# A second way to project sixteen meta tokens on TensorE, and one matmul for the router's sums

## The chip, the cores and the metric

The kernel runs on one core of one Trainium2 chip. The metric is the device time of one launch in microseconds. The kernel before takes 712.66 us (median of 3 runs, 712.54 to 715.22). The core has TensorE (PE, with its weight loads shown apart as PEld), VectorE (DVE), ScalarE (ACT), GpSimd (POOL) and SyncE (SP, which here only issues DMAs).

## The reference, cut to what matters

The model is one layer: 16 meta tokens are put in front of 512 tokens, all are projected by `w_in` (1024 x 3584) to seven groups of 512 columns, two mixers (a gated recurrence and a stick-breaking attention) work on these, an output projection and a layer norm follow, and a routed mixture of 16 experts with a second layer norm ends it.

```
h = concatenate([meta, x])                      # 16 + 512 rows of 1024, float32
proj = h @ w_in                                 # hq, hf, hi, hg, sq, sk, sv: 512 columns each
...
logits_g = xf @ w_rg + b_rg ;  logits_e = xf @ w_re + b_re     # xf: layer norm of the mixers' output
```

Of the meta tokens only four groups are used: hf (forget gates), hi (called hv in the kernel, the recurrence's values), sk and sv (attention keys and values). Outputs for the meta rows are dropped.

For the router, the kernel multiplies rows that are not yet normalised: with g and b the norm's gain and offset, it needs for each of the 20 logits the sum over the 1024 rows of b times the weight (added to the bias, tile `lgb`) and the sum over the rows of g times the weight (tile `nws`, to take off the mean). These two sums of 20 numbers, spread to all 128 partitions, are the "router's sums".

## The kernel before, in words

**Projections.** `projections` (L333 to L369) goes through the seven groups in the order hf, hq, hg, hv, sk, sv, sq. A group's weights come as two loads of 1 MB (`load_w`, the first group's in halves; raw tiles `raws`), each 1024 rows of contraction being 8 blocks (k = 0 to 7) of 128. Since one float32r pass rounds its operands, ACT makes a rounded copy of the weights (L329) and DVE or POOL the rest that is left (L124, L122 in `lo_sub`); x is split likewise (L200, L201). A product is then three float32r matmuls of 128 x 128 by 128 x 512: L128, L129 and L130 in `mm3`. For each k, four accumulators (pool `pj`, 4 banks of PSUM) get their three matmuls each.

**Meta tokens.** Their transposed values `xm` are the weights (stationary operand) of a matmul of their own, in 128 columns: columns 0 to 15 hold the rounded values, 32 to 47 the rest, the other columns zero. For each k of a group that needs them, L359 multiplies by the rounded weights and L360 by the rest of the weights, 512 moving columns each, into one bank of the pool `z`. At the group's end ACT copies partitions 32 to 47 (L366), DVE adds partitions 0 to 15 (L367), and a small routine stores the 16 rows: hf (L429) and sk (L382) by four transposes, hv by a copy on DVE, sv by one float32 matmul with `rep` (L413).

**Weaving.** After 27 steps (three groups) the remaining steps of the projections are woven with the recurrence's heads (`hg_head`), which use the pools `z`, `tr` and `oT`. The order on each engine is made by a scheduler from the order of the code and from what each instruction waits for; on the chip each engine goes through its list in order. Then follow the attention, woven with the output projection, the router, and 16 experts whose 96 MB of weights are streamed by SP.

**Router's sums.** `router_constants` (L303 to L321) runs among the projections. For the offset's sum, eight float32 matmuls (L315) have a column of b spread over 128 columns as weights and 20 moving columns; for the gain's sum, eight (L320) have a matrix of ones as weights and the scaled router weights as moving columns.

A float32 matmul that is not float32r shows as two records in the trace, each with a weight load of its own; a float32r matmul shows as one.

Of the kernel before, what the change touches and what calls it, by code (L numbers as in the profile page):

```python
# [9 lines left out]
F32 = mybir.dt.float32  # L10
F32R = mybir.dt.float32r
BF = mybir.dt.bfloat16
I32 = mybir.dt.int32
AF = mybir.ActivationFunctionType
OP = mybir.AluOpType
AX = mybir.AxisListType
PSUM = bass.MemoryType.PSUM

P = 128
D = 1024  # L20
T = 512
NM = 16
NT = T // P
KC = D // P
# [57 lines left out]
def hymba_kernel(ctx: ExitStack, tc: tile.TileContext, x, meta, w_in, lbnd, hgg, sbg, w_out, ln1g, ln1b,  # L82
                 wrg, brg, wre, bre, wg, wu, wd, ln2g, ln2b, out):
    nc = tc.nc
    V = nc.vector
# [4 lines left out]
    def f32(ap):  # L90
        return ap.bitcast(F32)
# [4 lines left out]
    const = ctx.enter_context(tc.tile_pool(name="const", bufs=1))  # L96
# [4 lines left out]
    def bank(tag, bufs, shape):  # L101
        return ps.tile(shape or [P, 512], F32, tag=tag, bufs=bufs, name=tag)
# [3 lines left out]
    trb = lambda shape=None: bank("tr", 1, shape)  # L106
# [7 lines left out]
    def big_tile(k, dt=F32, pool=None):  # L114
        return (pool or big).tile([P, 2048], dt, tag="b", name="b").rearrange("p (k n) -> p k n", k=k)
# [26 lines left out]
    att = ax_.enter_context(tc.tile_pool(name="att", bufs=1, side="right"))  # L142


    ident = const.tile([P, P], F32, name="ident")
# [10 lines left out]
    ones = upool.tile([P, P], F32, tag="ones", bufs=1, name="ones")  # L156
# [5 lines left out]
    def tt(tag="t", bufs=T_BUFS, n=528, parts=P):  # L162
        return att.tile([P, 528], F32, tag=tag, bufs=bufs, name=tag)[0:parts, 0:n]
# [8 lines left out]
    raws = {}  # L172
# [6 lines left out]
            nc.sync.dma_start(t[:, j * w:j * w + w], rap(w_in, (4 * half + j * w) * P * 3584 + GROUPS[n] * 512,  # L179
                                                         [[3584, P], [P * 3584, w], [1, 512]]))  # L180

    xm = big_tile(2, F32R)[:, 0].rearrange("p (k n) -> p k n", k=KC)
    nc.gpsimd.memset(f32(xm[:]), 0.0)
    mt = big_tile(2)[0:NM, 0, :]
    nc.scalar.dma_start(mt, meta)
    xr = [big_tile(2) for _ in range(2)]
# [4 lines left out]
    for i2 in range(2):  # L191
        xr_ = xr[i2]
        for i1 in range(2):
            i = 2 * i2 + i1
            for hf in range(2):
                p_ = pj([P, 4, P])
                for k in range(4):
                    nc.tensor.transpose(p_[:, k, :], xr_[:, i1, (4 * hf + k) * P:(4 * hf + k + 1) * P], ident)
                d_ = slice(i * P, (i + 1) * P)
                nc.scalar.activation(xhi_[hf][:, :, d_], p_, AF.Copy)  # L200
                x_last = V.tensor_sub(xlo_[hf][:, :, d_], p_, f32(xhi_[hf][:, :, d_])).ins  # L201
    p_ = trb([P, KC, NM])
    for k in range(KC):
        nc.tensor.transpose(p_[:, k, :], mt[:, k * P:(k + 1) * P], ident[:NM, :NM])
    nc.scalar.activation(xm[:, :, 0:NM], p_, AF.Copy)
    V.tensor_sub(xm[:, :, 32:32 + NM], p_, f32(xm[:, :, 0:NM]))

    prm = upool.tile([32, P], F32, tag="prm", bufs=1, name="prm")
    cp = const.tile([P, 32], F32, name="cp")
# [10 lines left out]
    for m in (16, 8, 4, 2, 1):  # L220
        t = upool.tile([P, P], I32, tag=f"lm{m}", bufs=1, name=f"lm{m}")
# [8 lines left out]
        lmask[m] = t  # L230
    identb = att.tile([P, P], BF, name="identb")
    maskb = att.tile([P, P], BF, name="maskb")
    rep = att.tile([NM, 8, NM], F32, name="rep")

    def bcast_row(t, src, eng):
        eng.dma_start(t, rap(src, 0, [[0, P], [1, D]]))
# [23 lines left out]
    wr, lgb, nws = small("wr", [KC, 20]), small("lgb", [20]), small("nws", [20])  # L260
# [22 lines left out]
    def feature_constants():  # L283
        V.tensor_copy(identb, ident)
        nc.gpsimd.memset(maskb, 0.0)
        nc.gpsimd.affine_select(out=maskb, in_=maskb, pattern=[[-1, P]], compare_op=OP.is_ge, fill=MASKED, base=-1,
                                channel_multiplier=1)
        V.tensor_copy(rep, ident[:NM, None, :NM].to_broadcast([NM, 8, NM]))
        for o, src, n in ((0, lbnd, 8), (8, hgg, 4), (12, sbg, 4), (16, ln1g, 8), (24, ln1b, 8)):
            nc.scalar.dma_start(prm[o:o + n], rap(src, 0, [[P, n], [1, P]]))  # L290
        p_ = trb([P, 32])
        nc.tensor.transpose(p_, prm, ident[:32, :32])
        V.tensor_copy(cp, p_)
        V.tensor_max(lbw[:, 0], cp[:, 0:4], cp[:, 4:8])
        V.tensor_sub(lbw[:, 1], cp[:, 0:4], lbw[:, 0])
        V.tensor_sub(lbw[:, 2], cp[:, 4:8], lbw[:, 0])
        nc.scalar.activation(lbw[:, 1:3], lbw[:, 1:3], AF.Exp)
        V.tensor_add(lbw[:, 2], lbw[:, 1], lbw[:, 2])
        V.reciprocal(lbw[:, 2], lbw[:, 2])
        V.tensor_mul(lbw[:, 3], lbw[:, 1], lbw[:, 2])  # L300
        V.tensor_scalar(lbw[:, 4], lbw[:, 3], -1.0, 1.0, op0=OP.mult, op1=OP.add)

    def router_constants():  # L303
        nc.gpsimd.iota(vt[:, :, 0], pattern=[[0, NT]], base=1, channel_multiplier=1, allow_small_or_imprecise_dtypes=True)
        nc.gpsimd.iota(vt[:, :, 1], pattern=[[P, NT]], base=0, channel_multiplier=0, allow_small_or_imprecise_dtypes=True)
        for j in range(2):
            V.tensor_copy(vals[:, :, :, j], vt[:, :, j:j + 1].to_broadcast([P, NT, NE]))
        nc.scalar.dma_start(wr[:, :, 0:4], rap(wrg, 0, [[4, P], [P * 4, KC], [1, 4]]))
        nc.scalar.dma_start(wr[:, :, 4:20], rap(wre, 0, [[16, P], [P * 16, KC], [1, 16]]))

        nc.scalar.dma_start(lgb[:, 0:4], rap(brg, 0, [[0, P], [1, 4]]))
        nc.scalar.dma_start(lgb[:, 4:20], rap(bre, 0, [[0, P], [1, 16]]))
        p_ = trb([P, 20])
        for k in range(KC):
            nc.tensor.matmul(p_, cp[:, 24 + k:25 + k].to_broadcast([P, P]), wr[:, k, :], start=(k == 0), stop=(k == KC - 1))  # L315
        V.tensor_add(lgb, p_, lgb)
        V.tensor_mul(wr, wr, cp[:, 16:24][:, :, None].to_broadcast([P, KC, 20]))
        p_ = trb([P, 20])
        for k in range(KC):
            nc.tensor.matmul(p_, ones, wr[:, k, :], start=(k == 0), stop=(k == KC - 1))  # L320
        V.tensor_scalar(nws, p_, -1.0, None, op0=OP.mult)  # L321


    latest = [None]
# [8 lines left out]
    def projections(uses):  # L333

        wt = {(0, 0): split_w(0, 0)}
        for n, (dmajor, evac, meta_evac) in enumerate(uses):
            acc = [pj() for _ in range(4)]
            pm = zb() if meta_evac else None
            for kk in range(4):
                if kk % 2 == 0 and n + 1 < len(uses):  # L340
                    load_w(n + 1, kk // 2)
                for k2 in range(2):
                    if k2 == 0:
                        whi, wlo = wt.pop((n, kk))
                        nxt = (n, kk + 1) if kk < 3 else (n + 1, 0)
                        if nxt[0] < len(uses):
                            wt[nxt] = split_w(*nxt)
                    k = 2 * kk + k2
                    wfl = slice(k2 * 512, (k2 + 1) * 512)
                    for c in range(4):  # L350
                        wsl = slice(k2 * 512 + c * P, k2 * 512 + (c + 1) * P)
                        xsl = slice(c * P, (c + 1) * P)
                        if dmajor:
                            mm3(acc[c], (whi[:, wsl], wlo[:, wsl]), (xhi[k], xlo[k]), k == 0, k == KC - 1)
                        else:
                            mm3(acc[c], (xhi[k][:, xsl], xlo[k][:, xsl]), (whi[:, wfl], wlo[:, wfl]),
                                k == 0, k == KC - 1)
                    if pm is not None:
                        nc.tensor.matmul(pm, xm[:, k, :], whi[:, wfl], start=(k == 0), stop=False)  # L359
                        nc.tensor.matmul(pm, xm[:, k, :], wlo[:, wfl], start=False, stop=(k == KC - 1))  # L360
                    yield 1
            for c in range(4):
                evac(c, acc[c])
            if pm is not None:
                t = tt(n=512, parts=NM)
                nc.scalar.activation(t, pm[32:32 + NM, :], AF.Copy)  # L366
                V.tensor_add(t, pm[0:NM, :], t)  # L367
                meta_evac(t)
            yield 1  # L369

# [8 lines left out]
    def mev_sk(t):  # L379
        p_ = trb([P, 4, NM])  # L380
        for c in range(4):
            nc.tensor.transpose(p_[:, c, :], t[:, c * P:(c + 1) * P], ident[:NM, :NM])  # L382
        for c in range(4):
            V.tensor_copy(skT[c][:, 0:NM], p_[:, c, :])

# [32 lines left out]
    hvm = ut(n=T)[0:NM]  # L418
# [7 lines left out]
    def mev_hf(t):  # L426
        p_ = trb([P, 4, NM])
        for h in range(4):
            nc.tensor.transpose(p_[:, h, :], t[:, h * P:(h + 1) * P], ident[:NM, :NM])  # L429
        for h in range(4):  # L430
            nc.scalar.activation(bt[h][:, 0:NM], p_[:, h, :], AF.Sigmoid)
            nc.scalar.activation(kt[h][:, 0:NM], p_[:, h, :], AF.Sigmoid, scale=-1.0)
# [10 lines left out]
        nc.scalar.activation(hvt[i], acc, AF.Copy)  # L443

    def mev_hv(t):
        V.tensor_copy(hvm, t)

    def ev_hg(h, acc):
        gt.append(ut(n=T))
# [406 lines left out]
    parts = []  # L856
    for e in range(NE):
        n = 4 if e == NE - 1 else 2 if e >= E_EARLY else 8
# [357 lines left out]
    for hf in range(2):  # L1216
        first_rows(hf, 0)
        p_ = p1_[hf]
# [67 lines left out]
    for e in range(NE):  # L1286
# [15 lines left out]
        if e == last - 1:  # L1302
            rr = []
            for i in range(0, NT, 2):
                t = big_tile(2)
# [170 lines left out]
```

## Time and profile before

| | before |
|---|---|
| median of 3 runs | 712.66 us |
| the profiled execution's own time | 715.65 us |
| its span, first to last instruction | 713.9 us |
| busy: PE / DVE / ACT / POOL | 661.7 / 525.2 / 412.3 / 155.0 us |
| mean granted clock of TensorE, share of full | 0.976 |

The profile is of one execution, which is 3.0 us above the median of the runs; 1.75 us of it lie around the span. A matmul's record is longer than the distance to the next one, because matmuls are pipelined: a record of 0.39 us is followed by the next after 0.23 us. What a matmul costs in a dense stretch is therefore the distance between starts, not the duration.

### The profile page before, as it was taken

The numbers are of one execution on the slowest core, as the hardware profiler recorded it, in microseconds if no ns is written. First come the engines' busy times: TensorE is split into PE (matmuls) and PEld (weight loads), VectorE is DVE, ScalarE is ACT, GpSimd is POOL, SyncE is SP. The second block draws the span as 40 slices with busy tenths as digits, with TensorE's granted clock in tenths as the row PEclk, the third lists the DMA queues.
The fourth block names the chain that finished last, engine by engine and source line by source line (L and its number), as shares of the span: only waits on it lengthen the run. The fifth ranks groups of instructions, "written<-read, shape, count | busy, mean of one in ns | idle before, by whom it ended". The sixth has DMA issues, their size and how long they took to land. (4 is left out here: it accounts for less than half of the span.)

```text
span 713.9 us, 9327 instructions
## 1 busy us (share of the span) xinstructions
PE 661.7 (93%) x3350; PEld 528.6 (74%) x3350; DVE 525.2 (74%) x833; ACT 412.3 (58%) x624; POOL 155.0 (22%) x177
## 2 busy tenths in 40 slices
PE   6999999999999999989977699999999999999963
PEld 5878878777877777778766588888778788787632
DVE  5433064666465696989877899999999999899384
ACT  5353253525262683856433587768688687697570
POOL 5201143343334100100011021413211141112201
PEclk9999999999999999999998799999999999999987
DMA  9431111030003790213576589999999999999631
GB/s 349 129 121 59 60 60 39 22 118 1 1 1 110 275 381 1 67 52 118 156 316 241 188 295 351 350 327 358 339 337 352 320 361 328 346 367 354 212 131 58
DMA packets 62307, 143.67 MB, mean 201 GB/s; under 512 B 7370, under 2 KB 7402, under 8 KB 62256
## 3 DMA queue, kind: packets, MB, share of 16 engines
q1 hardware_dynamic: 53312, 127.93, 49.6%
q0 software_dynamic: 5904, 12.82, 6.2%
q10 hardware_dynamic: 3040, 2.27, 1.0%
q8 instruction: 28, 0.46, 0.3%
q14 instruction: 23, 0.19, 0.1%
HBM read 137.01 MB, written 14.68 MB: 212 GB/s over the span
## 5 line engine op out<-in xcount | busy, mean ns | idle before, releaser
L908 DVE TENSOR_TENSOR b<-b 128x1024 fp32r<-128x1024 f32 x180 | 211.2, 1217 | 8.6 <-ACT b L907 8.1
L907 ACT ACTIVATE b<-b 128x1024 fp32r<-128x1024 f32 x180 | 177.3, 1054 | 13.2 <-SPq L1121 7.7
L128 PE MATMUL pj<-b 128*128 128x512 f32 x256 | 104.4, 411 | 0.3
L129 PE MATMUL pj<-b 128*128 128x512 f32 x256 | 101.9, 398 | 0.6 <-DVE b L124 0.6
L130 PE MATMUL pj<-b 128*128 128x512 f32 x256 | 102.5, 400 | 0.0
L128 PE MATMUL pj<-b,xh 128*128 128x512 f32 x224 | 89.9, 403 | 0.2 <-ACT b L907 0.2
L129 PE MATMUL pj<-b,xl 128*128 128x512 f32 x224 | 88.0, 394 | 0.0
L130 PE MATMUL pj<-b,xh 128*128 128x512 f32 x224 | 86.8, 403 | 0.5 <-DVE b L908 0.5
L974 POOL DMA_INDIRECT xg<-h1d,idx x15 | 20.3, 1354 | 184.3 <-DVE gate L971 82.7
L124 DVE TENSOR_TENSOR b<-b 128x1024 fp32r<-128x1024 f32 x24 | 33.1, 1392 | 33.8 <-ACT b L329 30.2
L128 PEld LDWEIGHTS pj<-b 128*128 128x128 f32 x256 | 48.9, 192 | 10.8 <-DVE b L201 0.7
L130 PEld LDWEIGHTS pj<-b 128*128 128x128 f32 x256 | 48.7, 190 | 10.8 <-issue 0.7
L129 PEld LDWEIGHTS pj<-b 128*128 128x128 f32 x256 | 48.9, 191 | 10.4 <-DVE b L124 0.9
L130 PEld LDWEIGHTS pj<-b,xh 128*128 128x128 f32 x224 | 42.3, 189 | 11.3 <-DVE b L908 2.6
L128 PEld LDWEIGHTS pj<-b,xh 128*128 128x128 f32 x224 | 42.5, 190 | 8.9 <-ACT b L907 1.5
L129 PEld LDWEIGHTS pj<-b,xl 128*128 128x128 f32 x224 | 42.6, 190 | 8.7
L329 ACT ACTIVATE b<-b 128x1024 fp32r<-128x1024 f32 x28 | 29.1, 1051 | 33.8 <-PE pj L130 15.2
L1021 POOL DMA_INDIRECT ad<-y,idx x14 | 39.2, 2802 | 42.7 <-ACT b L907 29.4
L626 ACT ACTIVATE zs<-zs 128x512 f32<-128x512 f32 x28 | 17.7, 631 | 49.1 <-POOL zs L625 49.0
L122 POOL TENSOR_TENSOR b<-b 128x1024 fp32r<-128x1024 f32 x8 | 19.4, 2430 | 91.9 <-ACT b L329 72.3
L624 POOL TENSOR_TENSOR zs<-u 128x256 f32<-128x256 f32 x28 | 22.2, 791 | 63.3 <-issue 25.8
L627 DVE TENSOR_TENSOR zs<-zs,u 128x256 f32<-128x256 f32 x28 | 13.3, 474 | 24.6 <-ACT zs L626 24.6
(357 smaller groups left out, 1310.9 us busy)
## 6 DMA issues: line engine op xcount, KB each, us to landing
b<-in_w_exp_gate_dram SPq DMA_DIRECT2D x32, 1024.0 KB, 8.7
b<-in_w_exp_up_dram SPq DMA_DIRECT2D x32, 1024.0 KB, 9.5
b<-in_w_exp_down_dram SPq DMA_DIRECT2D x32, 1024.0 KB, 8.3
b<-in_w_in_dram SPq DMA_DIRECT2D x12, 1024.0 KB, 5.2
b<-in_x_dram SPq DMA_DIRECT2D x8, 512.0 KB, 7.5
b<-in_w_out_dram SPq DMA_DIRECT2D x4, 1024.0 KB, 4.7
b<-in_w_in_dram SPq DMA_DIRECT2D x4, 512.0 KB
h1d<-b POOLq DMA_DIRECT2D x4, 512.0 KB, 3.0
```

Source lines behind the costliest of these rows:

```text
L122: nc.gpsimd.tensor_sub(dst, src, hi)
L124: V.tensor_sub(dst, src, hi)
L128: nc.tensor.matmul(acc, ah, bh, start=first, stop=False)
L129: nc.tensor.matmul(acc, al, bh, start=False, stop=False)
L130: nc.tensor.matmul(acc, ah, bl, start=False, stop=last)
L329: latest[0] = nc.scalar.activation(wt[:, 0], src, AF.Copy).ins
L624: nc.gpsimd.tensor_sub(xv[:, :, 0, :], ref, bv[:, :, 0, :])
L626: nc.scalar.activation(X, X, AF.Exp)
L907: latest[:] = (nc.scalar.activation(t[:, 0], raw, AF.Copy).ins, V.tensor_sub(t[:, 1], raw, f32(t[:, 0])).ins)
L908: V.tensor_sub(t[:, 1], raw, f32(t[:, 0])).ins)
L974: nc.gpsimd.indirect_dma_start(out=dst, out_offset=None, in_=h1d, in_offset=bass.IndirectOffsetOnAxis(ap=idx, axis=0), bounds_check=T - 1, ...
L1021: nc.gpsimd.indirect_dma_start(out=ad, out_offset=bass.IndirectOffsetOnAxis(ap=idx, axis=0), in_=y, in_offset=None, bounds_check=T - 1, oo ...
```

## The change

The meta tokens' weights `xm` become a float32 tile of 128 x 8 x 32 in the constants' pool (columns 16 to 31 of each block are zero), and no longer take one of the 14 buffers of the pool `big`. L359 and L360 go. Instead, after k = 3 and after k = 7, four float32 matmuls are issued, one for each of the last four k: 32 columns of weights, the raw float32 weights of the group as 512 moving columns, and each of the four writes its own 32 partitions of the bank (0, 32, 64, 96). So the four blocks' sums stand below each other, and are added only when the 16 rows are stored: ACT copies the whole 128 partitions, and the routine of each group multiplies by `fold`, a 128 x 16 matrix with ones where the row is i, 16 + i, 32 + i and so on. hf and sk then have four float32 matmuls in place of four transposes, hv has a matmul of 512 columns and a copy, sv keeps its one matmul with a `rep` of 128 rows in place of 16.

The router's sums over the eight row blocks are made on DVE (two products of 160 columns, two reductions), and one float32 matmul with the matrix of ones and 40 moving columns sums over the partitions.

```diff
-    xm = big_tile(2, F32R)[:, 0].rearrange("p (k n) -> p k n", k=KC)
+    xm = const.tile([P, KC, 32], F32, name="xm")
...
+    rep = att.tile([P, 8, NM], F32, name="rep")
+    fold = rep[:, 0, :]
+    V.tensor_reduce(fold, ident.rearrange("p (j i) -> p i j", i=NM), axis=AX.X, op=OP.add)
+    V.tensor_copy(rep[:, 1:8], rep[:, 0:1].to_broadcast([P, 7, NM]))
...
     nc.scalar.activation(xm[:, :, 0:NM], p_, AF.Copy)
-    V.tensor_sub(xm[:, :, 32:32 + NM], p_, f32(xm[:, :, 0:NM]))
...
-        for k in range(KC):
-            nc.tensor.matmul(p_, cp[:, 24 + k:25 + k].to_broadcast([P, P]), wr[:, k, :], start=(k == 0), stop=(k == KC - 1))
-        V.tensor_add(lgb, p_, lgb)
+        wb = tt(n=40 + KC * 20)
+        w_ = wb[:, 40:].rearrange("p (k n) -> p k n", k=KC)
+        V.tensor_mul(w_, wr, cp[:, 24:32][:, :, None].to_broadcast([P, KC, 20]))
+        V.tensor_reduce(wb[:, 0:20], w_.rearrange("p k n -> p n k"), axis=AX.X, op=OP.add)
         V.tensor_mul(wr, wr, cp[:, 16:24][:, :, None].to_broadcast([P, KC, 20]))
-        p_ = trb([P, 20])
-        for k in range(KC):
-            nc.tensor.matmul(p_, ones, wr[:, k, :], start=(k == 0), stop=(k == KC - 1))
-        V.tensor_scalar(nws, p_, -1.0, None, op0=OP.mult)
+        V.tensor_reduce(wb[:, 20:40], wr.rearrange("p k n -> p n k"), axis=AX.X, op=OP.add)
+        p_ = trb([P, 40])
+        nc.tensor.matmul(p_, ones, wb[:, 0:40], start=True, stop=True)
...
-                    if pm is not None:
-                        nc.tensor.matmul(pm, xm[:, k, :], whi[:, wfl], start=(k == 0), stop=False)
-                        nc.tensor.matmul(pm, xm[:, k, :], wlo[:, wfl], start=False, stop=(k == KC - 1))
+                    if pm is not None and k % 4 == 3:
+                        for j in range(4):
+                            nc.tensor.matmul(pm[32 * j:32 * j + 32], xm[:, k - 3 + j, :], raws[n, k // 4][:, j],
+                                             start=(k == 3), stop=(k == 7), skip_group_check=True)
...
-                t = tt(n=512, parts=NM)
-                nc.scalar.activation(t, pm[32:32 + NM, :], AF.Copy)
-                V.tensor_add(t, pm[0:NM, :], t)
+                t = tt(n=512)
+                nc.scalar.activation(t, pm, AF.Copy)
...
-            nc.tensor.transpose(p_[:, c, :], t[:, c * P:(c + 1) * P], ident[:NM, :NM])
+            nc.tensor.matmul(p_[:, c, :], t[:, c * P:(c + 1) * P], fold, start=True, stop=True)
...
     def mev_hv(t):
-        V.tensor_copy(hvm, t)
+        p_ = trb([P, 512])
+        nc.tensor.matmul(p_[0:NM], fold, t, start=True, stop=True)
+        V.tensor_copy(hvm, p_[0:NM])
```

The scheduler's lists change with it. The first place is the very start of PE's list. Before, the transposes of x (`pj<-ident,b`) and of the meta tokens (`tr<-ident,b`) stand first, then the first meta matmul of hf (`z<-b`) and the projection's own (`pj<-b`):

```order
L198 MATMUL pj<-ident,b 128x128 x16
L204 MATMUL tr<-ident,b 128x16 x8
L198 MATMUL pj<-ident,b 128x128 x16
L359 MATMUL z<-b 128x512
L128 MATMUL pj<-b 128x512 x4
L129 MATMUL pj<-b 128x512
L130 MATMUL pj<-b 128x512
```

Now all eight float32 matmuls of hf (`z<-b,xm`) stand there:

```order
L199 MATMUL pj<-ident,b 128x128 x16
L210 MATMUL tr<-ident,b 128x16 x8
L199 MATMUL pj<-ident,b 128x128 x8
L365 MATMUL z<-b,xm 32x512
L199 MATMUL pj<-ident,b 128x128 x8
L365 MATMUL z<-b,xm 32x512 x4
L128 MATMUL pj<-b 128x512
L129 MATMUL pj<-b 128x512
L365 MATMUL z<-b,xm 32x512 x3
L128 MATMUL pj<-b 128x512
```

They need only the raw weights and `xm`, so they have moved ahead of the split; the first stands ahead of the last eight transposes of x, and the last three after two of the projection's matmuls.

The second place is PE's list at the router's sums, in the middle of the projections. Before, the eight matmuls of the offset's sum (`tr<-wr,cp`) stand ahead of a meta pair, and the eight of the gain's sum (`tr<-wr,ones`) follow twelve matmuls later:

```order
L129 MATMUL pj<-b 128x512
L130 MATMUL pj<-b 128x512
L315 MATMUL tr<-wr,cp 128x20 x8
L359 MATMUL z<-b 128x512
L360 MATMUL z<-b 128x512
```

Now a single matmul stands in that region, behind 82 of the projection's matmuls that follow the parameters' transpose (before, the first eight came after 78):

```order
L129 MATMUL pj<-b 128x512
L130 MATMUL pj<-b 128x512
L323 MATMUL tr<-t,ones 128x40
L128 MATMUL pj<-b 128x512
L129 MATMUL pj<-b 128x512
```

Fifteen of the sixteen small matmuls are gone from the list, and so is the meta pair behind them. Of the six sets of four in hv, sk and sv, five stand as four in a row (`x4`), where before a pair L359, L360 followed each twelve of the projection's matmuls; in sk one set is parted, with one matmul first, twenty of the projection's, and then three.

## Rows read from the trace of the kernel before

**Rows 1.** Busy time by stage: stretch, length, each engine (count), clock, DMA share, GB/s.

```profile
16.00:40.00 24.00, 24.00 (x106) 19.87 (x107) 9.56 (x10) 9.26 (x12) 4.79 (x2) 1.00 0.50 169
40.00:98.00 58.00, 57.99 (x274) 48.00 (x273) 20.17 (x32) 23.90 (x39) 9.57 (x6) 1.00 0.22 65
98.00:165.00 67.00, 62.87 (x359) 51.75 (x357) 37.65 (x68) 27.42 (x52) 25.42 (x32) 1.00 0.17 56
165.00:235.00 70.00, 69.19 (x382) 55.14 (x381) 38.45 (x63) 30.09 (x58) 26.19 (x35) 1.00 0.12 40
235.00:410.00 175.00, 153.79 (x881) 124.92 (x880) 144.10 (x307) 95.21 (x183) 17.37 (x31) 0.94 0.49 179
410.00:650.00 240.00, 238.22 (x1156) 191.37 (x1155) 228.77 (x280) 188.51 (x223) 52.62 (x26) 1.00 0.97 340
```

**Rows 2.** PE's waits, 16 to 235 us: who, for whom, us in total, times, longest.

```profile
PE z L638 <- DVE aT L645: 2.1, 2, 1.5
PE z L636 <- DVE aT L616: 1.7, 1, 1.7
```

**Rows 3.** Tile z: the meta matmuls, ns min/median/max, first and last start.

```profile
L359 PE MATMUL z<-b x32: 387/389/791, 12.9 to 207.4; 128*128 128x512 f32 x32
L360 PE MATMUL z<-b x32: 388/390/398, 17.8 to 207.6; 128*128 128x512 f32 x32
```

**Rows 4.** PE's timeline at a pair of meta matmuls, and at hf's last: start us, us.

```profile
36.61 0.39 PE L359 MATMUL z<-b 128*128 128x512 f32 x1
36.84 0.39 PE L360 MATMUL z<-b 128*128 128x512 f32 x1
...
40.01 0.39 PE L360 MATMUL z<-b 128*128 128x512 f32 x1
```

**Rows 5.** PE's timeline, 686 us: two float32 matmuls of 512 columns, four records.

```profile
686.00 1.88 PE L1415 MATMUL z<-y,both 128*128 128x512 f32 x4
```

**Rows 6.** PE's timeline, 104 us: eight records of 64 columns.

```profile
103.89 0.65 PE L636 MATMUL z<-zs 128*64 128x64 f32 x8 [1.66 <-DVE aT L616]
```

**Rows 7.** PE's timeline at the start, 9 to 16 us.

```profile
9.58 3.67 PE L198 MATMUL pj<-ident,b 128*128 128x128 f32 x16
12.91 0.78 PE L359 MATMUL z<-b 128*128 128x512 f32 x1
13.48 1.76 PE L128 MATMUL pj<-b 128*128 128x512 f32 x4
15.87 0.50 PE L129 MATMUL pj<-b 128*128 128x512 f32 x1 [0.63 <-DVE b L124]
```

**Rows 8.** ACT's timeline at the start: the first split of the weights.

```profile
11.23 1.05 ACT L329 ACTIVATE b<-b 128x1024 fp32r<-128x1024 f32 x1
```

**Rows 9.** PE's timeline at the router's sums, 63 to 70 us.

```profile
63.05 1.86 PE L315 MATMUL tr<-wr,cp 128*128 128x20 f32 x16
...
65.07 0.39 PE L360 MATMUL z<-b 128*128 128x512 f32 x1
...
68.02 1.86 PE L320 MATMUL tr<-wr,ones 128*128 128x20 f32 x16
...
70.04 0.40 PE L129 MATMUL pj<-b 128*128 128x512 f32 x1
```

**Rows 10.** PE's timeline at hf's transposes and at a matmul on 32 rows.

```profile
42.96 0.39 PE L128 MATMUL pj<-b 128*128 128x512 f32 x1
43.35 0.42 PE L429 MATMUL tr<-ident,t 16*128 16x16 f32 x4
...
44.04 0.40 PE L130 MATMUL pj<-b 128*128 128x512 f32 x1
...
44.73 0.40 PE L130 MATMUL pj<-b 128*128 128x512 f32 x1
45.06 0.24 PE L292 MATMUL tr<-ident,prm 32*128 32x32 f32 x1
45.23 0.50 PE L128 MATMUL pj<-b 128*128 128x512 f32 x1
```

More of the change, by code (lines that the diff above doesn't have):

```diff
@@ L180, in load_w @@
                                                          [[3584, P], [P * 3584, w], [1, 512]]))
-    xm = big_tile(2, F32R)[:, 0].rearrange("p (k n) -> p k n", k=KC)
-    nc.gpsimd.memset(f32(xm[:]), 0.0)
+    xm = const.tile([P, KC, 32], F32, name="xm")
+    nc.gpsimd.memset(xm, 0.0)
     mt = big_tile(2)[0:NM, 0, :]
@@ L232, in hymba_kernel @@
     maskb = att.tile([P, P], BF, name="maskb")
-    rep = att.tile([NM, 8, NM], F32, name="rep")
     def bcast_row(t, src, eng):
@@ L287, in feature_constants @@
                                 channel_multiplier=1)
-        V.tensor_copy(rep, ident[:NM, None, :NM].to_broadcast([NM, 8, NM]))
         for o, src, n in ((0, lbnd, 8), (8, hgg, 4), (12, sbg, 4), (16, ln1g, 8), (24, ln1b, 8)):
@@ L312, in router_constants @@
         nc.scalar.dma_start(lgb[:, 4:20], rap(bre, 0, [[0, P], [1, 16]]))
-        p_ = trb([P, 20])
-        for k in range(KC):
-            nc.tensor.matmul(p_, cp[:, 24 + k:25 + k].to_broadcast([P, P]), wr[:, k, :], start=(k == 0), stop=(k == KC - 1))
-        V.tensor_add(lgb, p_, lgb)
+        wb = tt(n=40 + KC * 20)
+        w_ = wb[:, 40:].rearrange("p (k n) -> p k n", k=KC)
+        V.tensor_mul(w_, wr, cp[:, 24:32][:, :, None].to_broadcast([P, KC, 20]))
+        V.tensor_reduce(wb[:, 0:20], w_.rearrange("p k n -> p n k"), axis=AX.X, op=OP.add)
         V.tensor_mul(wr, wr, cp[:, 16:24][:, :, None].to_broadcast([P, KC, 20]))
-        p_ = trb([P, 20])
-        for k in range(KC):
-            nc.tensor.matmul(p_, ones, wr[:, k, :], start=(k == 0), stop=(k == KC - 1))
-        V.tensor_scalar(nws, p_, -1.0, None, op0=OP.mult)
+        V.tensor_reduce(wb[:, 20:40], wr.rearrange("p k n -> p n k"), axis=AX.X, op=OP.add)
+        p_ = trb([P, 40])
+        nc.tensor.matmul(p_, ones, wb[:, 0:40], start=True, stop=True)
+        V.tensor_add(lgb, p_[:, 0:20], lgb)
+        V.tensor_scalar(nws, p_[:, 20:40], -1.0, None, op0=OP.mult)
     latest = [None]
@@ L428, in mev_hf @@
         for h in range(4):
-            nc.tensor.transpose(p_[:, h, :], t[:, h * P:(h + 1) * P], ident[:NM, :NM])
+            nc.tensor.matmul(p_[:, h, :], t[:, h * P:(h + 1) * P], fold, start=True, stop=True)
         for h in range(4):
```

## The prediction

> **What bounds the kernel now.** I read the busy time by stage first. From 16 to 98 us PE is busy all the time, and from 98 to 235 us 94% and 99%, while DVE, ACT and the DMA engines are far from full [rows 1]. The reader is to see that a PE instruction taken out of these 220 us shortens them by the distance it took, and that nothing else is near to filling them. The waits of PE come second: in 16 to 235 us the longest are 2.1 and 1.7 us, both for tiles that DVE writes in the recurrence's heads [rows 2]. They could grow when PE has less to do between two levels of a head. From 410 to 650 us the DMA engines are 97% busy [rows 1]; from 98 to 235 us they are at 17 and 12%. The expert weights start only when the projections' buffers come free, so the loaded stage should move as a whole when the projections end earlier. That is a reading, and a rival below takes the other side.
>
> Third, the timeline of PE gives prices. The next instruction starts 0.227 us after a float32r matmul of 512 columns (36.61 to 36.84 [rows 4]), whatever the 0.39 us of its record. Two float32 matmuls of 512 columns take four records in 1.88 us, the last one 0.59 long [rows 5]: (1.88 - 0.59) / 3 = 0.43 us a record, so 0.86 us a matmul, nearly four times a float32r one.
>
> **The meta matmuls of hv, sk and sv.** Of 64 meta matmuls [rows 3], 48 belong to these groups: 48 x 0.227 = 10.9 us go, all in the stretch that PE bounds. In come 24 float32 matmuls on 32 columns, in six sets. No row shows two matmuls side by side on different columns, so I bound a set of four. It can't take less than one matmul's two records, 0.86 us, since each block must send 512 columns through its own 32 in the same passes as any float32 matmul. It can't take more than four in turn, 3.44 us. Between lies a chain in which a matmul's second record holds back the next block's first: 5 x 0.43 = 2.15 us. The nearest row is of eight records of 64 columns in 0.65 us, the last 0.27 long: 0.054 us from start to start [rows 6]. So sending a record and its weight load costs at most 0.054 us and doesn't bound; what spaces records is the columns they need, and the four blocks need different ones. I take 0.86 us, the lower end.
>
> A change of shape on the array has a price too. A matmul on 32 rows starts 0.33 us after its forerunner in place of 0.23, and the record behind it is 0.50 long in place of 0.39 [rows 10]: 0.1 us at each side, 0.2 us a set. The Trainium skill says that a change of tiling mode drains TensorE (TensorEngine Tiling (Array Packing), Key Properties) and gives no time for it. By a whole drain at both sides, taken as a record less the distance, 0.39 - 0.23 = 0.16 us, the sets would cost 0.8 us more in all; the rows say 0.1, and I keep that.
>
> Five whole sets: 5 x 1.06 = 5.3 us. The one that is parted costs twice 1.06 = 2.1 us. Sum 7.4, against 10.9: **-3.5 us**. By the chain: 5 x 2.35 + 1.06 + (4 x 0.43 + 0.2) = 14.7, so +3.8. In turn: 24 x 0.86 + 7 x 0.2 = 22.0, so +11.1.
>
> **The meta matmuls of hf, at the start.** Here the order moves. Before, x's last 16 transposes start at 9.58 and take 0.23 us each; the dense stream begins at 15.87, after waits for DVE's splits, and hf's last meta matmul starts at 40.01 [rows 7, 4], so hf ends at 40.24. The four L128 from 13.48 are about 0.46 us apart [rows 7], twice the later distance: I read this as the lower of the two levels, or waits, although the granted clock says full for these stages. Now the first float32 matmul stands ahead of x's last eight transposes. Its weights have landed by 11.23, when ACT starts to split them [rows 8], so it doesn't hold PE for the DMA; it takes 1.7 us at the low pace: transposes to 11.2, this to 12.9, the last eight to 14.7. Four more side by side, 1.06: 15.7. Two of the projection's (0.45): 16.2. Three more, 1.06: 17.3. Then the 94 left of hf's 96: 94 x 0.227 = 21.3, so hf ends at 38.6: **-1.6 us**. By the chain (2.35 and 1.92 in place of the two 1.06) it ends at 40.8, +0.5; in turn (3.64 and 2.78) at 42.9, +2.7. All of it replaces 16 x 0.227 = 3.6 us of matmuls and some idle time.
>
> **The router's sums.** The eight matmuls of the first sum run from 63.05 to 65.07 - 0.23 = 64.84, so 1.79 us, 0.112 a record; the other eight from 68.02 to 70.04 - 0.23 = 69.81, the same [rows 9]. One matmul of two records stays, some 0.3 us: **-3.3 us**. The new products and reductions lie on DVE, which is busy for 20 us of the 58 [rows 1]; were they late, PE would wait at that one matmul for at most about a microsecond, with the projection's matmuls queued behind it.
>
> **The sums over the blocks.** hf's four transposes with their change of shape run from 42.96 + 0.23 = 43.19 to 44.04 - 0.23 = 43.81, of which 0.16 is a wait for DVE [rows 10]: 0.46 us. Four float32 matmuls with weight loads of 128 columns are eight records of 0.112, with the changes 1.0 us: +0.5, for hf and for sk. hv gains a matmul of 512 columns, 1.06 us. Sum **+2.1 us**. sv's matmul stays what it was. L206's and L367's DVE work is saved where DVE waits anyway, and costs nothing.
>
> **Buffers and waits.** One buffer of `big` and some time of the pool `z` come free, and the raw weights are held until the float32 matmuls have read them. The loads they hold up run a group (24 us) ahead with the DMA engines at 12 to 22% [rows 1], so I cost both at nothing; that cover would be gone only if a load were issued 20 us late. PE's waits in the heads [rows 2] grow by what is saved between two levels: I take +0.6, of at most some 3.5.
>
> **Sum.** -3.5 - 1.6 - 3.3 + 2.1 + 0.6 = -5.7 us. The profiled execution took 715.65 us and would take 709.95; it lies 3.0 us above the median of the runs, and the same off 712.66 gives **707 us**.
>
> **Rivals.**
>
> *A chain on the array.* PE's records start in the order of its list, and a block's second record needs the columns that its first still uses. If nothing behind a waiting record may start, a set costs five records. Then +3.8 + 0.5 - 3.3 + 2.1 = +3.1: 715.8 us. The Trainium skill says that matmuls start and end strictly in program order (TensorE: Matmul & The Clock Gate, What overlaps and what doesn't), which would lead here; its packing gain there, 2.38 times for three column blocks, speaks for side by side. For it: no record in the timelines starts ahead of its turn. Against: a waiting record might queue at its own columns.
>
> *In turn.* The four blocks don't overlap at all, each float32 matmul costs 0.86 us as on the whole array [rows 5], and 24 + 8 of them replace 64 of 0.227. Then +11.1 + 2.7 - 3.3 + 2.1 = +12.6: 725.3 us, slower. For it: the trace holds no pair of matmuls that overlap in this way. Against: [rows 6], columns and not issue set the distance. It decides from about 2.45 us a set on: at the chain's 2.35 the sum is +3.1, and there it passes +3.6, half a percent.
>
> *Swallowed later.* The projections end earlier, and the stage from 410 us, 97% DMA [rows 1], ends when it did. Then 712.7. Against: the DMA engines are at 49% between 235 and 410 us, so loads there wait for buffers that PE and DVE free.
>
> **How the numbers follow.** Side by side 0.40 (its own range 703 to 710: the waits and the clock, 0.94 from 235 to 410 us, can each move it by 2 to 3 us); chain 0.32 (711 to 719); in turn 0.20 (720 to 729); swallowed 0.08. A difference under 0.5%, 3.6 us, can't be told from none. Faster: nearly all of the first, 0.38, and 0.03 of the chain, 0.41. Same: the rest of the first, 0.20 of the chain and the swallowed, 0.30. Slower: 0.09 of the chain and all in turn, 0.29. The range reaches from 702 to 720: it leaves out most of in turn.
>
> **What would show it.** In the profile after: a set of four's records. Side by side: eight records within about 1.1 us, and the next projection matmul 1.1 us after the set's first start. Chain: 2.2 to 2.4. In turn: 3.4 to 3.6. The router's one matmul shows as two records; hf ends near 38.6, the last projection about 6 us earlier than now, and the stage at 97% DMA starts earlier by as much. Wrong would be: a set over 2 us, PE idle between 98 and 235 us grown by over 3 us, or the expert stage starting no earlier.

## The result and the profile after

The changed kernel takes 706.31 us (median of 4 runs, 703.20 to 708.31) against 712.75 us (4 runs): a ratio of 0.9882, interval [0.9833, 0.9931]. The forecast was 707. In five runs on another chip the ratio was 0.9852, [0.9822, 0.9883]. The profiled execution took 708.31 us (span 706.6) against 715.65, so 7.3 us less.

First, what a set of four is. The timeline of PE of the changed kernel (columns as in [rows 4]), in two windows; the first closes at 96.2 us, 0.23 us after the set's first start, the second behind the set:

```profile
95.65 0.39 PE L130 MATMUL pj<-b 128*128 128x512 f32 x1
95.97 0.64 PE L365 MATMUL z<-b,xm 128*32 128x512 f32 x4
```

```profile
95.97 1.07 PE L365 MATMUL z<-b,xm 128*32 128x512 f32 x8
```

The reader is to see four records in the short window and eight in the whole set: four records start together (they end 0.64 us after the first start), the other four follow together, and eight records take 1.07 us, hardly more than the 0.86 us and a tail that two records of one matmul take by [rows 5]. I take the first four to be the first records of the four blocks: on the same columns records start 0.43 us apart (experiment 3), so four that start together lie on different ones.

The start, where [rows 7] stood:

```profile
9.64 1.97 PE L199 MATMUL pj<-ident,b 128*128 128x128 f32 x8
11.53 1.92 PE L365 MATMUL z<-b,xm 128*32 128x512 f32 x2
13.38 1.25 PE L199 MATMUL pj<-ident,b 128*128 128x128 f32 x8
14.56 1.07 PE L365 MATMUL z<-b,xm 128*32 128x512 f32 x8
15.56 0.50 PE L128 MATMUL pj<-b 128*128 128x512 f32 x1
15.89 0.40 PE L129 MATMUL pj<-b 128*128 128x512 f32 x1
16.22 1.06 PE L365 MATMUL z<-b,xm 128*32 128x512 f32 x6
17.21 0.50 PE L128 MATMUL pj<-b 128*128 128x512 f32 x1
```

The first, single matmul takes 1.92 us, at half pace; four and three blocks then take 1.07 and 1.06. Three in company cost what four do.

hf's sums over the blocks and the router's matmul, in place of [rows 10] and [rows 9]:

```profile
38.65 0.96 PE L434 MATMUL tr<-rep,t 128*128 128x16 f32 x8
39.46 0.48 PE L128 MATMUL pj<-b 128*128 128x512 f32 x1
39.78 0.39 PE L129 MATMUL pj<-b 128*128 128x512 f32 x1
...
62.04 0.31 PE L323 MATMUL tr<-t,ones 128*128 128x40 f32 x2
62.18 0.48 PE L128 MATMUL pj<-b 128*128 128x512 f32 x1
62.49 0.40 PE L129 MATMUL pj<-b 128*128 128x512 f32 x1
```

PE's waits between 16 and 235 us, where [rows 2] stood; and the first level of the first head, where PE waits longest:

```profile
PE z L643 <- DVE aT L623: 2.0, 1, 2.0
PE z L645 <- DVE zs L635: 0.6, 2, 0.4
PE oT L693 <- DVE t L687: 0.4, 1, 0.4
PE z L645 <- DVE aT L652: 0.2, 1, 0.2
```

```profile
99.05 1.05 PE L643 MATMUL z<-zs 128*64 128x64 f32 x8 [2.01 <-DVE aT L623]
100.03 0.80 PE L128 MATMUL pj<-b 128*128 128x512 f32 x1
100.63 0.63 PE L129 MATMUL pj<-b 128*128 128x512 f32 x1
101.06 0.63 PE L130 MATMUL pj<-b 128*128 128x512 f32 x1
```

Behind the wait of 2.0 us the records stand 0.43 us apart in place of 0.23. The stages around show why; the columns are those of [rows 1]:

```profile
95.00:99.00 4.00, 2.04 (x13) 0.70 (x11) 3.17 (x6) 2.23 (x6) 0.32 (x1) 1.00 0.39 114
99.00:102.40 3.40, 3.35 (x14) 2.79 (x15) 0.23 (x1) 1.01 (x2) 1.24 (x2) 0.51 0.45 174
102.40:105.80 3.40, 3.40 (x20) 2.96 (x19) 0.53 (x2) 0.53 (x2) 0.20 (x1) 0.99 0.00 0
```

The granted clock is 0.51 for 3.4 us, the 1.2 GHz level: some 1.7 us lost (an estimate: half of 3.4 us) that the kernel before didn't lose (1.00 from 16 to 235 us [rows 1]). PE had been busy for 2.04 of the 4 us ahead.

Last, what came of the gain. The last sum of squares of the recurrence's heads marks the projections' end; the transposes of the experts' rows (tile xg) mark the expert stage. Before, then after:

```profile
L470 PE MATMUL z<-t,ones x8: 592/631/697, 131.1 to 233.2; 128*128 128x512 f32 x8
L1042 PE MATMUL z<-ident,xg x120: 270/272/328, 391.7 to 650.8; 128*128 128x128 f32 x120
```

```profile
L477 PE MATMUL z<-t,ones x8: 592/631/697, 127.3 to 225.8; 128*128 128x512 f32 x8
L1049 PE MATMUL z<-ident,xg x120: 270/272/329, 384.7 to 643.6; 128*128 128x128 f32 x120
```

7.4 us are gained by the projections' end, and 7.0 and 7.2 at the expert stage's begin and end. All that was gained early arrives, although the DMA engines are nearly full in the expert stage: the stage moved as a whole. That rules out the rival of a gain swallowed later.

### The profile page after: what moved, and what is told of

It is laid out like the page before. It is cut to its first block, busy times and chain, and to the rows that moved or that the text cites. A ratio compares the mean times of both kernels' runs of the same rounds, so it can differ in the third digit from the quotient of the medians.

```text
span 706.6 us, 9286 instructions
## 1 busy us (share of the span) xinstructions
PE 656.9 (93%) x3330; PEld 516.3 (73%) x3330; DVE 526.1 (74%) x832; ACT 412.2 (58%) x624; POOL 150.9 (21%) x177
## 5 line engine op out<-in xcount | busy, mean ns | idle before, releaser
L914 ACT ACTIVATE b<-b 128x1024 fp32r<-128x1024 f32 x180 | 177.3, 1054 | 13.1 <-PE pj L130 11.2
L1028 POOL DMA_INDIRECT ad<-y,idx x14 | 34.7, 2478 | 42.3 <-ACT b L914 29.4
```

Of the source, the lines that this page charges most:

```text
L914: latest[:] = (nc.scalar.activation(t[:, 0], raw, AF.Copy).ins, V.tensor_sub(t[:, 1], raw, f32(t[:, 0])).ins)
L1028: nc.gpsimd.indirect_dma_start(out=ad, out_offset=bass.IndirectOffsetOnAxis(ap=idx, axis=0), in_=y, in_offset=None, bounds_check=T - 1, oo ...
```

## The experiments

Kernels of the first four runs share one chip (before: 715.88 us), those of the last four another (before: 715.48 us). Ratios are to the kernel before on the same chip.

**1. The router's sums alone.** The kernel before with the new code of `router_constants`.

```diff
-        for k in range(KC):
-            nc.tensor.matmul(p_, cp[:, 24 + k:25 + k].to_broadcast([P, P]), wr[:, k, :], ...)
...
+        nc.tensor.matmul(p_, ones, wb[:, 0:40], start=True, stop=True)
```

> The kernel before with the router's sums alone changed (products and reductions on DVE, one matmul). Theory (each part gives what PE's timeline prices it at): 3.3 us less, 709.4. Rival (the meta part gains nothing and the router's part and the freed buffer are the whole gain): 706 to 707, as much as the whole change. Second rival (DVE's new work is late and PE waits for it): over 711.

Measured: 714.50 us, ratio 0.9986, [0.9971, 1.0002]. The theory's 3.3 us would be 0.9954, outside the interval. In the profile the projections end at 230.8 us, 2.4 before the kernel before. This execution had a stretch of the lower clock behind 15 us, and hf's last meta matmul starts at 40.55 us in place of 40.01 [rows 4]:

```profile
L471 PE MATMUL z<-t,ones x8: 592/632/697, 128.8 to 230.8; 128*128 128x512 f32 x8
```

```profile
15.30 0.63 PE L130 MATMUL pj<-b 128*128 128x512 f32 x1
15.73 0.63 PE L129 MATMUL pj<-b 128*128 128x512 f32 x1
...
40.55 0.39 PE L361 MATMUL z<-b 128*128 128x512 f32 x1
```

With these 0.5 us and 0.3 us more of waits behind the start (5.2 in place of 4.9), PE's part is 3.2 us: the price holds there. The rival is refuted (this part is not the whole gain), but so is the price as a gain of the whole kernel: about 1 us reaches the median. In the profiled execution it is lost behind the projections, between 235 and 410 us (where the granted clock is 0.93 in place of 0.94) and in the expert stage:

```profile
L1043 PE MATMUL z<-ident,xg x120: 270/272/331, 390.9 to 652.0; 128*128 128x128 f32 x120
```

The expert stage begins 0.8 us earlier than before and ends 1.2 later. Over all runs the mean granted clock is 0.974 here and 0.976 in the kernel before on this chip, which is worth up to 1.9 us (an estimate: 0.0026, the difference before rounding, of 714). So the clock may hold most of the rest; that it does is not shown.

**2. The meta part alone.** The whole change with the old `router_constants`.

> The whole change with the router's sums as they were before (sixteen small float32 matmuls). Theory: 6.4 us gain of the whole less the router's 3.3, so 709 to 710. Rival (the meta part gains nothing by itself): 712 to 713. In the profile a set of four takes 1.0 to 1.1 us under the theory.

Measured: 709.37 us, 0.9916, [0.9882, 0.9949], a gain of 3.7 to 8.4 us: the larger part, and the rival falls. The theory's 3.1 us was too little: it took what PE's timeline gives for the router's sums from the whole, and they brought less (experiment 1). That the time lies at the 709 to 710 that it named is chance, since the kernel before takes 715.88 us on this chip and not 712.66. The projections end at 227.2 us, 6.0 earlier than before:

```profile
L476 PE MATMUL z<-t,ones x8: 592/631/697, 128.7 to 227.2; 128*128 128x512 f32 x8
```

It has the same wait of 2.0 us at the first level as the whole change, and no low stretch behind it:

```profile
101.99 0.65 PE L642 MATMUL z<-zs 128*64 128x64 f32 x8 [2.01 <-DVE aT L622]
102.57 0.50 PE L128 MATMUL pj<-b 128*128 128x512 f32 x1
102.91 0.40 PE L129 MATMUL pj<-b 128*128 128x512 f32 x1
```

So the whole change, 1.4 us earlier at the projections' end, would be 3.1 earlier without its low stretch: about the router's 3.3 is there on PE.

**3. The same columns for all four blocks.**

```diff
-    nc.tensor.matmul(pm[32 * j:32 * j + 32], xm[:, k - 3 + j, :], raws[n, k // 4][:, j],
-                     start=(k == 3), stop=(k == 7), skip_group_check=True)
+    nc.tensor.matmul(pm[0:32], xm[:, k - 3 + j, :], raws[n, k // 4][:, j],
+                     start=(k == 3 and j == 0), stop=(k == 7 and j == 3), skip_group_check=True)
...
```

> The whole change, but all four row blocks of a set go through the same 32 columns and add up in the same 32 partitions; the sums over blocks then use 32 rows. Result and number of matmuls are the same. Theory (the gain hangs on the four blocks running side by side on different columns): a set takes four matmuls in turn, 3.4 to 3.6 us in place of 1.07, six sets after the start cost 6 x 2.4 = 14 us, the start some 4: 722 to 726. Rival (32 columns in themselves make a float32 matmul cheap, whichever columns): a set stays at about 1.1 us and the time at 706.

Measured: 720.54 us, 1.0087, [1.0060, 1.0114], slower than before. The same set of hv, and the instruction behind it:

```profile
98.78 3.62 PE L365 MATMUL z<-b,xm 128*32 128x512 f32 x8
102.33 0.68 PE L644 MATMUL z<-zs 128*64 128x64 f32 x8
```

3.55 us to the next start, where the whole change has records of 1.07 us in all. A set's instructions, their number and their widths are equal; only the columns differ, and with them the partitions that they write. Records here start 0.43 us apart, as those on the whole array do [rows 5], so writing the same partitions adds nothing to that. Four different column blocks make the gain, not narrow matmuls in themselves. It is also the rival "in turn" as a kernel, slower as that said, though by 6 us by the ratio (4.7 by the medians) and not by 13; the theory's 722 to 726 was too much as well. Part of the difference is in the waits: the longest here is 0.4 us, and all together are 1.0 us where the kernel before has 5.5, so the long sets seem to cover them. The start was cheaper too, since this execution had the full clock there, and the mean granted clock of the six runs is 0.980 where the kernel before has 0.976. The buffer of `big` that `xm` gives back is free here too, and the kernel is slower than before; no run takes that buffer by itself.

**4. hv's meta sums in another bank.**

```diff
-            pm = zb() if meta_evac else None
+            pm = (otb() if n == 3 else zb()) if meta_evac else None
```

> The whole change, with the meta sums of the group hv in the bank oT in place of one of the two banks of z. At 97 to 99 us of the changed kernel PE waits 2.0 us for DVE to free a bank of z (L643 for L623), and the granted clock is at its lower level for some 3.4 us around it. Theory (the wait is for the bank, and the clock falls with the wait): the wait goes, the clock stays up, 2 to 4 us less than the whole change: 702.5 to 704.5. Rival (the wait is for DVE's place in its list, whichever bank): the wait stays, 706. Second rival (the wait goes, but the clock falls elsewhere or the heads give it back later): 705 to 707.

Measured: 703.18 us, 0.9838, [0.9813, 0.9862]. Its waits and the projections' end:

```profile
PE z L645 <- DVE zs L635: 0.6, 2, 0.4
PE oT L693 <- DVE t L687: 0.4, 1, 0.4
PE tr L452 <- ACT t L372: 0.3, 1, 0.3
```

```profile
L477 PE MATMUL z<-t,ones x8: 592/632/697, 123.3 to 220.8; 128*128 128x512 f32 x8
```

The wait of 2.0 us is gone, and the granted clock stays at 1.00 up to 235 us. The wait was for the bank: with hv's sums in one bank of z, the head's first level needs the one that L623 still reads. The projections end 5.0 us before the whole change's, but not all of that is the bank's. This execution had the full clock at the start already, and hf ends sooner than in the whole change (38.65):

```profile
10.49 1.05 PE L365 MATMUL z<-b,xm 128*32 128x512 f32 x2
11.47 1.09 PE L199 MATMUL pj<-ident,b 128*128 128x128 f32 x8
...
36.59 0.96 PE L434 MATMUL tr<-rep,t 128*128 128x16 f32 x8
```

Without these 2.1 us it is 2.9 us. About 1.7 are the low stretch that is missing and 1.9 the waits (1.3 us in all in place of 3.2); about 1 us goes the other way, since in this order hv's first set is parted too, with one matmul at 60.21 us and three at 94.98. That the low stretch hangs on the wait is not shown, since experiment 2 has the wait without it. Nor do these runs show that the version beats the whole change: its interval overlaps both of the change's (0.9833 to 0.9931 and 0.9822 to 0.9883). Experiment 8 has the same edit on the chip of experiment 5.

**5. The whole change again.** No edit.

> The whole change, unedited, beside the next three on one chip and against the kernel before. Theory (the meta part's 6 us and the router's 3 us less what a low stretch of the clock takes): a ratio of 0.988 to 0.991. Rival (the two parts don't add up): a ratio near 0.9916, that of the meta part alone, or over it.

Measured: 705.48 us, 0.9852, [0.9822, 0.9883]. Its profile has the low stretch again at 99.3 us, as in the first. The ratio is a little below the theory's 0.988 to 0.991, whose lower end is still inside the interval. It is below that of the meta part alone, but that was on another chip, and the intervals overlap; that the parts add up in the median isn't shown.

**6. The bank held as long as before.**

```diff
-                    if pm is not None and k % 4 == 3:
+                    if pm is not None and k % 4 == 0:
...
-                            nc.tensor.matmul(pm[32 * j:32 * j + 32], xm[:, k - 3 + j, :], raws[n, k // 4][:, j],
-                                             start=(k == 3), stop=(k == 7), skip_group_check=True)
+                            nc.tensor.matmul(pm[32 * j:32 * j + 32], xm[:, k + j, :], raws[n, k // 4][:, j],
+                                             start=(k == 0), stop=(k == 4), skip_group_check=True)
```

> The whole change, but the sets of four are issued at k = 0 and k = 4 in place of k = 3 and k = 7, so that a bank of z is held from the beginning of a group, as in the kernel before. Number and kind of matmuls are the same. Theory (PE waits less in the heads after the change, 3.1 us in place of 5.0 between the first level and the projections' end, because the bank is held for half as long): PE's waits return to about 5 us, 2 us slower than the whole change. Rival (the waits fell because DVE has no more L367 and less to do, or by chance): waits stay at about 3 us, the same time as the whole change.

Measured: 709.55 us, 0.9919, [0.9890, 0.9947], 4 us over the whole change on the same chip. Its waits:

```profile
PE z L645 <- DVE aT L652: 2.8, 2, 2.6
PE z L643 <- DVE aT L623: 1.8, 1, 1.8
```

They return to 4.6 us from 3.2: most of what they were before. (One more set is parted in this order, which costs about 1 us besides.) So DVE's lighter load, which this kernel has too, is not what lowered the waits. What did is when the sums are issued and take their bank. That it is the length of the hold alone is not shown: the order of the list changes with it, the first level's wait is much the same (1.8 us, 2.0 in the whole change), and the wait of 2.6 us that came back lies at 145 us, where the whole change holds a bank for sk as well. The 4 us are not all waits either. The projections' end here and in experiment 5:

```profile
L477 PE MATMUL z<-t,ones x8: 592/631/679, 126.7 to 226.9; 128*128 128x512 f32 x8
L477 PE MATMUL z<-t,ones x8: 592/632/697, 127.4 to 225.9; 128*128 128x512 f32 x8
```

Only 1.0 us of the 3.5 between the two profiled executions (711.28 and 707.75) stands there, since the 1.4 of waits and the 1 of the parted set are set against the low stretch of about 1.7, which only experiment 5 has. The other 2.5 come behind the projections, where the granted clock is lower (0.93 in place of 0.94 from 235 to 410 us).

**7. The bank alone, in the kernel before.** The edit of experiment 4 there.

> The kernel before, with the meta sums of hv in the bank oT in place of one of z, nothing else. Theory (the second bank of z is what the first level of the first head waits for): the wait of 1.7 us for DVE (L636 for L616) goes, 1.5 to 3 us less than before. Rival (DVE's place in its list sets it): no change. If it gains as much as it did in the changed kernel, the bank's gain and the change's gain are independent.

Measured: 713.96 us, 0.9975, [0.9955, 0.9995]: about 1.8 us (0.4 to 3.2), as the theory said. The wait of L636 for L616 is gone and all waits are 3.1 us in place of 5.5; its projections end at 230.4 us, 2.8 earlier:

```profile
L470 PE MATMUL z<-t,ones x8: 592/631/697, 129.6 to 230.4; 128*128 128x512 f32 x8
```

In the changed kernel the same edit gave 2.9 there without the start, some 1.7 of it the low stretch.

**8. The other bank, and transposes for the sums.**

```diff
-        p_ = trb([P, 4, NM])
+        p_ = trb([P, 4, P])
         for c in range(4):
-            nc.tensor.matmul(p_[:, c, :], t[:, c * P:(c + 1) * P], fold, start=True, stop=True)
+            nc.tensor.transpose(p_[:, c, :], t[:, c * P:(c + 1) * P], ident)
         for c in range(4):
-            V.tensor_copy(skT[c][:, 0:NM], p_[:, c, :])
+            V.tensor_reduce(skT[c][:, 0:NM], p_[:, c, :].rearrange("p (j i) -> p i j", i=NM), axis=AX.X, op=OP.add)
...
```

> The whole change with hv's meta sums in the bank oT, and with the sums over the blocks of hf and sk made by four transposes of 128 x 128 (one record each) and a reduction on DVE, in place of four float32 matmuls with fold (two records each). Theory: 4 records of 0.11 us less, twice, so 0.9 us less than with the bank alone, a ratio of 0.981 to 0.984 against before. Rival (the reductions on DVE come late and the head or the attention waits for them): as the bank alone, 0.984, or slower.

Measured: 702.63 us, 0.9829, [0.9800, 0.9858], the fastest of all. hf's sums now take 0.2 us less (39.61 - 0.23 - 38.65 = 0.73 in place of 0.90), where the theory had half of its 0.9:

```profile
38.65 0.60 PE L434 MATMUL tr<-ident,t 128*128 128x128 f32 x4
39.28 0.50 PE L128 MATMUL pj<-b 128*128 128x512 f32 x1
39.61 0.40 PE L129 MATMUL pj<-b 128*128 128x512 f32 x1
```

Its projections end at 222.6 us, 3.3 before those of experiment 5, with hf's sums beginning at 38.65 in this one too. Against experiment 4 the ratios' difference is inside the intervals; that the transposes themselves gain in the whole is not shown. That the version beats the change is likely (702.63 against 705.48 on one chip), as experiment 4 would have it, but the two intervals overlap (0.9800 to 0.9858, 0.9822 to 0.9883).

## Why the prediction was right

The direction, the mechanism and the size were right, by the sum that the traces give at the projections' end: 7.4 us of the 7.3 that the execution gained, against 5.7 forecast. (The medians moved by 6.4 us, and the ratio 0.9882 stands for 8.4; with four runs each, these don't part the 5.7 from the 7.4.) By its steps:

- *Side by side, taken at the lower end of the bounds.* Right: a set is 1.07 us of records, as forecast 1.06, and the next instruction starts 1.00 us after it (14.56 to 15.56). Experiment 3 shows what the upper end would have been. The argument from [rows 6], that columns and not issue space the records, held. The chain, the rival with 0.32, is refuted by the short window above: a block's second record doesn't hold back the next block's first. Nothing in the trace of before told the two apart, so the lower end was a choice at a chance of 0.40, and that it came out is luck in part; the stated range of 702 to 720 would have held the chain as well.
- *The start, -1.6.* Right: hf's last matmul is followed by L434 at 38.65 against a forecast end of 38.6, so 40.24 - 38.65 = 1.6 us. The first matmul at half pace (1.92 us) came as expected. (The prediction ends the eight transposes ahead of it at 11.2, where its 0.23 us each would give 11.4; it starts at 11.53.) The 1.6 hangs on the clock of the execution: with the full clock at the start, experiment 4 has L434 at 36.59, 3.65 us before the 40.24.
- *The router's sums, -3.3.* Right on PE: L323 takes 62.49 - 0.23 - 62.04 = 0.22 us of the 3.58 that were. But by itself it brings about 1 us to the whole (experiment 1); why no more stays open.
- *The sums over the blocks, +2.1.* Right for hf: 39.78 - 0.23 - 38.65 = 0.90 us for 0.46 before.
- *PE's waits, +0.6.* Wrong, also in sign. They fell from 5.5 us in all (2.1, 1.7, 0.6, 0.5, 0.4 and 0.2) to 3.2; 0.6 of the 5.5 lie at the start and belong to its term, so it is -1.7 where I took +0.6. I reasoned that less work on PE between two levels leaves more to wait, and costed the time of the pool z that comes free "at nothing", when it was a gain: the sums now take a bank only from k = 3 on. Experiments 4 and 7 take hv's sums out of z, and the waits fall in both kernels; experiment 6 takes the bank as early as before and they return, though its order changes too. (The 2.1 us that the prediction calls the longest wait are two waits together; the longest single ones were 1.7 and 1.5 [rows 2].)
- *The clock.* I allowed 2 to 3 us from 235 us on, and named none ahead. The low stretch at 99 us costs about 1.7 us, and takes back what the waits gave.

So the forecast of 707 is near partly because two misses, -2.3 in the waits and +1.7 in the clock, nearly cancel: -5.7 - 2.3 + 1.7 = -6.3 of the -7.4 at the projections' end. About 1 us more is left over. It stands behind hf's end, where the six sets and the sums lie; which of them were priced too high, or whether it is something else, I have not parted.

## What to carry to other kernels

Where a matmul has few weight columns, price several of them on different column blocks as one, and look in the trace for first records that start together; put them on the same columns once to see what hangs on it. When a change moves who holds a bank of PSUM and for how long, cost the hold and not only the instruction: here one line that moves a group's sums to a bank of another pool took away the longest wait of PE. And where runs of one kernel differ by 3 to 5 us, compare the clock at the start and behind PE's waits before a difference of 2 us is believed.

## What the runs showed of the hardware that I had not expected

- Four float32 matmuls on four column blocks run as two rounds of four records, 1.07 us, and three as long (1.06). The Trainium skill gives 2.38 times for three column blocks of 32 (TensorE: Matmul & The Clock Gate, Part 3); here, by the records of a set in experiment 3 and in the whole change, 3.62 / 1.07 is about 3.4 times for four in float32.
- By 96.2 us four records of a set have started and the other four not, and the set takes 1.07 us. The Trainium skill states that matmuls start and end strictly in program order (TensorE: Matmul & The Clock Gate, What overlaps and what doesn't); read as I read it for the chain, that would have made a set 2.2 us. In which order the eight stand in the list on the chip, no run here shows, so the measurement refutes my reading and not the statement.
- The clock at the start differs between executions of nearly the same code: the first float32 matmul takes 1.92 us in the whole change's profile and 1.05 in experiment 4's, and hf ends 2.1 us apart.
- A wait of 2.0 us at PE was followed by 3.4 us at the 1.2 GHz level in both profiles of the whole change, and by none in the meta part alone, with the same wait, nor in experiment 1, whose wait at that level is 2.1 us. What decides between them stays open.
